# Row exponents of a gated delta-rule layer: from TensorE products to a trip through device memory

## The chip, the core and the metric

The kernel runs on one core of a Trainium2 chip. The metric is device time in microseconds (us) of one execution. The core has a matrix engine (TensorE, PE in the profile, with PEld for its weight loads), VectorE (DVE), ScalarE (ACT), GpSimd (POOL), a queue processor (SyncE, SP) and 16 DMA engines. Each engine works through its own list of instructions in order, and semaphores hold it where another engine's or a transfer's result is needed. DMA is issued from SP and from POOL here.

## The reference, cut to what matters

The model is a bidirectional encoder with two layers over 512 tokens of width 1024: first gated delta rule, then gated linear attention, each followed by an MLP. The change touches the delta-rule layer alone. It has 8 heads and two directions; each direction is computed in chunks:

```python
decay_mat = exp(where(causal, gc[..., :, None] - gc[..., None, :], -inf))
a_mat = where(strict, einsum('bhncd,bhnsd->bhncs', k * beta, k) * decay_mat, 0)
sol = triangular_solve(a_mat + eye, concat([v * beta, k * beta * exp(gc)]))
qk = einsum('bhncd,bhnsd->bhncs', q, k) * decay_mat
q_dec = q * exp(gc)
...
v_new = u_c - w_c @ state
o = q_dec @ state + qk @ v_new
```

`gc` is the running sum of log decays in a chunk. Every entry of `decay_mat` needs an exponent that belongs to its row plus one that belongs to its column, and `q_dec` needs one factor for each token.

## The kernel before, in words

Tokens are cut into 4 chunks of 128 (`NT = 4`, `P = 128`). `gdn` makes 8 `GdnHead` objects and emits, for step i, `recur` (the recurrence) of head i-2, `solve` of head i-1, `project` with `rows` of head i, and `finish` of head i-2. This is only the order in which code is written. A scheduler then merges the instructions into one list for each engine, by priorities and its own estimate of when things are ready; those lists are fixed in the program. Three heads are thus in work at once.

- `project` makes k, q, v and a gate z of the head: 24 products each (`pjk`, `pjq`, `pjv`, `pjz`), of a split weight `wh`, `wl` with a split x. Weights come through `wst` (3 buffers) on the SP queue.
- `rows` transposes k and q (`ktp`), sums their squares and makes, with tokens on partitions, the exponents: `rw` holds for each token, chunk and direction the exponent of its row, `cj` that of its column.
- `solve` makes k k^T (`kk`) and the decay matrix `E`, transposed: partition is the column's token, the free axis the row's. So `rw` is needed along the free axis and the same on all 128 partitions. Before, it is split into three bf16 parts (`rs`), transposed on TensorE (`rtp`, copied to `rt`, 6 x 512), and spread over the partitions by a product with the selector `sel` (`ep`, one PSUM bank per direction). From `ep` ScalarE makes exp for q (`qd`), then a second product adds the mask `mi` (-1e30 where the row is not later) to the same bank, and ScalarE makes `E`, with `cj` as its bias, in 8 pieces of 128 x 128. `E` times `kk` is `at`, its half-precision form `ath`, the 4 x 4 diagonal blocks `a4`; the solve starts with the products `hp` and goes on by doubling block sizes (`lv`, casts into `pz` and `Dd`), then `nw`, and `qk` (times `E`: `qke`).
- `recur` runs the states through products `m1`, `m2`, `m3` with ScalarE and VectorE between them, and makes the output `op`. `finish` normalises it on ScalarE (`fo`), transposes it on TensorE (`otp`) and applies the gate.

The PSUM pool has 8 banks: `ch` 2, `pj` 3, `tp` 1, `ac` 2; `ep`, `hp`, `lv`, `nw` and `qk` use the two of `ac`.

Of the kernel before, what the change touches and what calls it, by code (L numbers as in the profile page):

```python
# [17 lines left out]
P = 128  # L18
S = 512
# [1104 lines left out]
class GdnConst:  # L1124


    def __init__(self, c, pool, w_in, a_log, dt_bias, conv_w, norm_g, x):
        self.c, self.pool = c, pool
# [46 lines left out]
    def masks(self):  # L1175
        c, pool = self.c, self.pool
        G = c.nc.gpsimd
        self.idb = pool.tile([P, P], BF16, name="idb", bufs=1)
        G.tensor_copy(self.idb, c.ident)
# [3 lines left out]
        sf = pool.tile([6, 2, P], F32, name="self", tag="E", bufs=2)  # L1183
        G.memset(sf, 0.0)
        for s in range(3):
            G.affine_select(out=sf, in_=sf, compare_op=ALU.not_equal, fill=1.0, base=-2 * s,
                            pattern=[[-1, 2], [0, P]], channel_multiplier=1)
# [141 lines left out]
def gdn(c, w_in, conv_w, a_log, dt_bias, norm_g, w_out, ln_g, ln_b, x, w_next):  # L1329
    tc, nc = c.tc, c.nc  # L1330
    with c.banks(ch=2, pj=3, tp=1, ac=2), tc.tile_pool(name="gdn", bufs=1) as pool:
        g = GdnConst(c, pool, w_in, a_log, dt_bias, conv_w, norm_g, x)
# [9 lines left out]
        def load_z(hf):  # L1342
            if hf:
                tl = pool.tile([P, NT, S], F32, name="z", tag="sil", bufs=3)
            else:
                tl = heads[-1].next.kq
                more = [heads[-1].t2(tag, n).rearrange("p n i -> p (n i)") for tag, n in (("kt", 3), ("qd", 4))]
# [30 lines left out]
class GdnHead:  # L1378
# [75 lines left out]
    def rows(self, done):  # L1454
# [21 lines left out]
        rw = c.small.tile([P, NT, 2], F32, name="rw", tag="rw")  # L1476
# [4 lines left out]
        rs = c.small.tile([P, NT, 6], BF16, name="rsp", tag="rsp")  # L1481
        r1 = c.small.tile([P, NT, 2], F32, name="r1", tag="r1")
        V.tensor_copy(rs[:, :, 0:2], rw)
        V.tensor_tensor(r1, rw, rs[:, :, 0:2], ALU.subtract)
        V.tensor_copy(rs[:, :, 2:4], r1)
        V.tensor_tensor(r1, r1, rs[:, :, 2:4], ALU.subtract)
        V.tensor_copy(rs[:, :, 4:6], r1)
        rtp = self.bank("rtp", BF16, tag="tp")
        for n in range(NT):
            T.transpose(rtp[:6, n, :], rs[:, n, :], g.idb)  # L1490
        self.rt = pool.tile([6, S], BF16, name="rt", tag="rt", bufs=2)
        A.copy(self.rt, rtp[:6, :, :].rearrange("p n i -> p (n i)"))
# [17 lines left out]
    def solve(self, done):  # L1510
# [11 lines left out]
        eps, self.qd = [], []  # L1522
        for d in range(2):
            ps = self.bank("ep")
            T.matmul(ps, g.sel[:, d, :], self.rt, start=True, stop=True)
# [3 lines left out]
            self.qd.append(x)  # L1529
            eps.append(ps)  # L1530
# [7 lines left out]
        with c.in_order(mybir.EngineType.PE):  # L1538
            for d in (1, 0):
                T.matmul(eps[d], g.idb, g.mi[d].unsqueeze(1).to_broadcast([P, NT, P]), start=False, stop=True, skip_group_check=True)  # L1540
        for d, ps in enumerate(eps):
            e = self.t2("E", 2)
# [266 lines left out]
```

## Time and profile before

| | |
|---|---|
| runs | 1338.26, 1338.63, 1339.11 us |
| median | 1338.63 us |
| profiled execution | 1339.1 us as recorded with the trace |
| its span, first to last instruction | 1335.5 us |
| TensorE's mean granted clock | 0.997 of full speed |
| busy over the span: PE, DVE, ACT, POOL | 98%, 82%, 60%, 9% |
| moved by DMA | 154.35 MB, mean 116 GB/s |

The page gives busy times of the engines, groups of equal instructions with the idle time ahead of them and what ended it, the DMA issues with the time from issue to landing, and the chain of work that ended last. L with a number is a line of the kernel. A duration of a matmul is from its start to its modelled end; matmuls overlap, so that the distance between two starts tells what one of them costs the engine. The delta layer takes about 410 us of the span, and the rest (two MLPs and the linear attention) is the same code before and after.

### The profile page before, as it was taken

The numbers are of one execution on the slowest core, as the hardware profiler recorded it, in microseconds if no ns is written. First come the engines' busy times: TensorE is split into PE (matmuls) and PEld (weight loads), VectorE is DVE, ScalarE is ACT, GpSimd is POOL, SyncE is SP. The second block draws the span as 40 slices with busy tenths as digits, with TensorE's granted clock in tenths as the row PEclk, the third lists the DMA queues.
The fourth block names the chain that finished last, engine by engine and source line by source line (L and its number), as shares of the span: only waits on it lengthen the run. The fifth ranks groups of instructions, "written<-read, shape, count | busy, mean of one in ns | idle before, by whom it ended". The sixth has DMA issues, their size and how long they took to land.

```text
span 1335.5 us, 22220 instructions
## 1 busy us (share of the span) xinstructions
PE 1313.2 (98%) x8629; PEld 1122.0 (84%) x8629; DVE 1097.8 (82%) x1802; ACT 800.3 (60%) x1590; POOL 124.2 (9%) x177
## 2 busy tenths in 40 slices
PE   9999999999999999999999999999999999999996
PEld 8777787787777989999998888888889899999985
DVE  7797877888768878989988887967879679989888
ACT  4767666767643655666566754654456466566656
POOL 4000000000000910100102100000001001101011
PEclk9999999999999999999999999999999999999998
DMA  6221111211232684775748542222327476767566
GB/s 184 67 68 40 47 48 48 64 37 68 72 96 74 201 174 140 164 183 148 165 126 176 137 119 64 64 64 64 95 64 201 120 185 138 161 172 147 155 138 146
DMA packets 155660, 154.35 MB, mean 116 GB/s; under 512 B 7723, under 2 KB 122531, under 8 KB 155555
## 3 DMA queue, kind: packets, MB, share of 16 engines
q1 hardware_dynamic: 143779, 110.85, 28.1%
q0 software_dynamic: 11776, 42.08, 16.1%
q8 instruction: 68, 1.11, 0.3%
q14 instruction: 37, 0.30, 0.1%
HBM read 113.99 MB, written 2.10 MB: 87 GB/s over the span
## 4 chain that ended last, share of the span: by engine, by line
PE 87%; DVE 5%; ACT 5%; issue 1%; DMA 1%; DVEq 0%; POOL 0%; ACTq 0%; POOLq 0%
PE pX L123 3%; PE pX L122 3%; PE pX L124 3%; PE fx L124 3%; PE fx L123 3%; PE fx L122 3%; PE pjv L122 3%; PE pjv L123 3%; PE pjv L124 3%; PE m L1699 3%; PE pj L123 3%; PE pj L124 3%; PE pj L122 3%; PE fyz L122 2%; PE fyz L124 2%; PE fyz L123 2%
## 5 line engine op out<-in xcount | busy, mean ns | idle before, releaser
L96 ACT CAST wh<-wst 128x1024 fp32r<-128x1024 f32 x150 | 157.5, 1050 | 106.7 <-PE fyz L123 31.4
L101 DVE TENSOR_TENSOR wl<-wst,wh 128x1024 fp32r<-128x1024 f32 x148 | 182.3, 1232 | 46.4 <-ACT wh L96 45.4
L101 DVE TENSOR_TENSOR w2l<-w2r,w2h 128x1024 fp32r<-128x1024 f32 x92 | 112.3, 1220 | 28.4 <-ACT w2h L96 28.3
L96 ACT CAST w2h<-w2r 128x1024 fp32r<-128x1024 f32 x94 | 98.4, 1048 | 56.7 <-PE pX L124 24.8
L401 POOL DMA_DIRECT2D w2r<-w2r x56 | 48.4, 891 | 500.5 <-DVE w2l L101 176.3
L96 ACT CAST ah<-h 128x1024 fp32r<-128x1024 f32 x56 | 58.8, 1050 | 51.8 <-PE pZ L123 23.2
L450 DVE TENSOR_TENSOR wst<-wst 128x512 f32<-128x512 f32 x110 | 73.0, 682 | 0.2
L101 DVE TENSOR_TENSOR al<-h,ah 128x1024 fp32r<-128x1024 f32 x56 | 68.4, 1221 | 5.2 <-ACT ah L96 5.2
L123 PE MATMUL pX<-w2l,ah 128*128 128x512 f32 x168 | 66.2, 394 | 0.0
L122 PE MATMUL pX<-w2h,ah 128*128 128x512 f32 x168 | 66.0, 393 | 0.0
L124 PE MATMUL pX<-w2h,al 128*128 128x512 f32 x168 | 65.7, 391 | 0.0
L123 PE MATMUL pj<-xtl,wh 128*128 128x256 f32 (+1 forms) x192 | 64.7, 338 | 0.2 <-DVE xtl L188 0.2
L124 PE MATMUL pj<-xth,wl 128*128 128x256 f32 (+1 forms) x192 | 64.5, 337 | 0.0
L122 PE MATMUL pj<-xth,wh 128*128 128x256 f32 (+1 forms) x192 | 64.3, 337 | 0.1
L122 PE MATMUL pjv<-wh,xth 128*128 128x512 f32 x128 | 54.4, 425 | 0.0
L124 PE MATMUL pjv<-wh,xtl 128*128 128x512 f32 x128 | 50.2, 392 | 0.0
L123 PE MATMUL pjv<-wl,xth 128*128 128x512 f32 x128 | 50.0, 391 | 0.0
L124 PE MATMUL fx<-xh,wl 128*128 128x256 f32 x176 | 49.8, 283 | 0.0
L124 PE MATMUL fyz<-xh,wl 128*128 128x256 f32 x176 | 49.7, 282 | 0.0
L122 PE MATMUL fyz<-xh,wh 128*128 128x256 f32 x176 | 49.7, 282 | 0.0
L124 PE MATMUL fx<-xth,wl 128*128 128x256 f32 x176 | 49.7, 282 | 0.0
L123 PE MATMUL fx<-xtl,wh 128*128 128x256 f32 x176 | 49.7, 282 | 0.0
(528 smaller groups left out, 4303.5 us busy)
## 6 DMA issues: line engine op xcount, KB each, us to landing
wst<-in_mlp_w SPq DMA_DIRECT2D x68, 512.0 KB, 5.1
w2r<-in_mlp_w SPq DMA_DIRECT2D x60, 512.0 KB, 4.4
w2r<-w2r POOLq DMA_DIRECT2D x56, 512.0 KB, 5.6
wst<-in_a_w_in SPq DMA_DIRECT2D x32, 512.0 KB, 4.1
wst<-in_b_w_in SPq DMA_DIRECT2D x32, 256.0 KB, 3.1
wst<-in_a_w_out SPq DMA_DIRECT2D x8, 512.0 KB, 3.6
wst<-in_b_w_in SPq DMA_DIRECT2D x8, 512.0 KB, 4.0
wst<-in_b_w_out SPq DMA_DIRECT2D x8, 512.0 KB, 3.7
```

The source lines that it names most:

```text
L96: h = nc.scalar.copy(hi, src)
L101: self.halves = h, nc.vector.tensor_tensor(lo, src, hi.bitcast(F32), ALU.subtract)
L122: mm(ps, ah, bh, start=start, stop=False, **kw)
L123: mm(ps, ah, bl, start=False, stop=False, **kw)
L124: self.last_mm = mm(ps, al, bh, start=False, stop=stop, **kw)
L401: nc.gpsimd.dma_start(blocks[a + (q,)], blocks[b + (q,)], accum_op=ALU.add)
L450: plus = lambda a, b: V.tensor_tensor(a, a, b, ALU.add)
L1699: T.matmul(ps[:, d, :], *ops(d), start=True, stop=True)
```

## The change

The exponents no longer pass TensorE. SP copies the mask, which lies in device memory four times over (`later`, made and written once at the start), into `E`, and writes `rw` element by element as 8 rows of 128 into a small buffer in device memory (`row`). POOL then issues two transfers, each of which reads those 8 rows once for every partition: the first adds them onto the mask in `E`, the second puts them into `qd` as they are. ScalarE's exponentials work in place on `E` and `qd`. `qd` is one tile for both directions; its product with q becomes one VectorE instruction. The split into bf16 parts, the transposes, the copy `rt` and the four products per head are gone, with `sel`, `idb` and `mi`. A load of x late in the layer gets another half of a `qd` tile.

```diff
 class GdnConst.masks
-        self.sel = pool.tile([6, 2, P], BF16, name="sel", bufs=1)
-        G.tensor_copy(self.sel, sf)
-        self.mi = [pool.tile([P, P], BF16, name=f"mi{d}", bufs=1) for d in range(2)]
+        later = pool.tile([P, 2, P], F32, name="later", bufs=1)
         for d in range(2):
-            t = pool.tile([P, P], F32, name="tri", tag="cf", bufs=2)
-            self.tri(t, d, False, 0.0, NEG)
-            G.tensor_copy(self.mi[d], t)
+            self.tri(later[:, d, :], d, False, 0.0, NEG)
+        self.later = self.dram.tile([P, 2, NT, P], F32, name="laterd", bufs=1)
+        for n in range(NT):
+            G.dma_start(self.later[:, :, n, :], later)
...
 GdnHead.rows
-        rw = c.small.tile([P, NT, 2], F32, name="rw", tag="rw")
+        rdn = c.small.tile([P, 2, NT], F32, name="rw", tag="rw")
+        rw = rdn.rearrange("p d n -> p n d")
...
-        V.tensor_copy(rs[:, :, 0:2], rw)
-        V.tensor_tensor(r1, rw, rs[:, :, 0:2], ALU.subtract)
-        V.tensor_copy(rs[:, :, 2:4], r1)
-        V.tensor_tensor(r1, r1, rs[:, :, 2:4], ALU.subtract)
-        V.tensor_copy(rs[:, :, 4:6], r1)
-        rtp = self.bank("rtp", BF16, tag="tp")
-        for n in range(NT):
-            T.transpose(rtp[:6, n, :], rs[:, n, :], g.idb)
-        self.rt = pool.tile([6, S], BF16, name="rt", tag="rt", bufs=2)
-        A.copy(self.rt, rtp[:6, :, :].rearrange("p n i -> p (n i)"))
+        row = g.dram.tile([2 * NT, P], F32, name="row", tag="row", bufs=3)
+        self.e = pool.tile([P, 2, NT, P], F32, name="E", tag="E", bufs=2)
+        self.qd = pool.tile([P, 2, NT, P], F32, name="qd", tag="qd", bufs=2)
+        c.nc.sync.dma_start(self.e, g.later)
+        with c.nc.allow_non_contiguous_dma("one column to a row"):
+            c.nc.sync.dma_start(row.rearrange("u p -> p u"), rdn.rearrange("p d n -> p (d n)"))
+        every = row.rearrange("u p -> (u p)").partition_broadcast(P)
+        c.nc.gpsimd.dma_start(self.e.rearrange("p d n i -> p (d n i)"), every, accum_op=ALU.add)
+        c.nc.gpsimd.dma_start(self.qd.rearrange("p d n i -> p (d n i)"), every)
...
 GdnHead.solve
-        for d in range(2):
-            ps = self.bank("ep")
-            T.matmul(ps, g.sel[:, d, :], self.rt, start=True, stop=True)
-            x = self.t2("qd", 4)
-            A.activation(x, ps, AF.Exp)
-            V.tensor_tensor(x, self.kq[:, 1, :].rearrange("p (n i) -> p n i", n=NT), x, ALU.mult)
+        x = self.qd
+        A.activation(x, x, AF.Exp)
+        V.tensor_tensor(x, self.kq[:, 1, :].rearrange("p (n i) -> p n i", n=NT).unsqueeze(1).to_broadcast([P, 2, NT, P]),
+                        x, ALU.mult)
...
-        with c.in_order(mybir.EngineType.PE):
-            for d in (1, 0):
-                T.matmul(eps[d], g.idb, g.mi[d].unsqueeze(1).to_broadcast([P, NT, P]), start=False, stop=True, skip_group_check=True)
-        for d, ps in enumerate(eps):
-            e = self.t2("E", 2)
+        for d in range(2):
+            e = self.e[:, d, :, :]
             for n in range(NT):
-                A.activation(e[:, n, :], ps[:, n, :], AF.Exp, bias=self.cj[:, n, d:d + 1])
+                A.activation(e[:, n, :], e[:, n, :], AF.Exp, bias=self.cj[:, n, d:d + 1])
```

The scheduler makes new lists. Three places of them follow; the numbers behind names tell tiles apart.

On TensorE, where head 5's `kk` and head 3's `otp` stand, the list of before has the two selector products (`ep`, with the loads of `sel`) between `otp` and `kk`:

```order
L1757 MATMUL otp_3536<-ident_70,fo_3531 128x128
L1525 LDWEIGHTS sel_355
L1525 MATMUL ep_3654<-rt_3431,sel_355 128x512
L1525 LDWEIGHTS sel_355
L1525 MATMUL ep_3659<-rt_3431,sel_355 128x512
L122 MATMUL pjq_3977<-xth_107,wh_3973 128x512
L123 MATMUL pjq_3977<-xtl_108,wh_3973 128x512
L1699 MATMUL m2_3552<-vt_3550,xf_3305 128x128 x2
L1519 MATMUL kk_3649<-sil_2858 128x128 x4
```

and the list of now, at the same `otp` of head 3, goes on to the recurrence (`m2`) at once:

```order
L123 MATMUL pjk_3814<-xtl_110,wh_3810 128x512
L124 MATMUL pjk_3814<-xth_109,wl_3811 128x512
L1741 MATMUL otp_3421<-ident_70,fo_3416 128x128
L122 MATMUL pjk_3814<-xth_109,wh_3810 128x512
L1741 MATMUL otp_3421<-ident_70,fo_3416 128x128 x2
L123 MATMUL pjk_3814<-xtl_110,wh_3810 128x512
L1741 MATMUL otp_3421<-ident_70,fo_3416 128x128
L1683 MATMUL m2_3437<-vt_3435,xf_3197 128x128 x2
```

The products for the exponents are gone, and `kk` of head 5 now stands ahead of `otp`, 24 rows above it.

On ScalarE at the same place, from head 5's `neg` to its exponentials, the list of before:

```order
L197 ACTIVATE rsy_3521<-rsy_3521 128x4
L96 CAST wh_4100<-wst_4098 128x1024
L1492 COPY rt_3431<-rtp_3426 6x512
L1753 ACTIVATE fo_3531<-op_3017,ors_3519 128x128 x4
L1402 ACTIVATE sil_3475<-pjk_3941,cw_304 128x512
L1687 COPY vt_3550<-ktp_3545 128x512
L1527 ACTIVATE qd_3656<-ep_3654 128x512
```

and the list of now:

```order
L1496 ACTIVATE fq_3324<-c0_3325,bias2_79 128x4
L196 ACTIVATE rsy_3406<-oss_3398,bias1_77 128x4
L96 CAST wh_3929<-wst_3927 128x1024
L1435 COPY sil_3360<-pjz_3372 128x512
L197 ACTIVATE rsy_3406<-rsy_3406 128x4
L1671 COPY vt_3435<-ktp_3430 128x512
L1528 ACTIVATE E_3312<-E_3312,cj_3309 128x128 x6
L1515 ACTIVATE qd_3313<-qd_3313 128x1024
L1737 ACTIVATE fo_3416<-op_2921,ors_3404 128x128 x4
L1528 ACTIVATE E_3312<-E_3312,cj_3309 128x128 x2
```

The exponentials of `E` and `qd`, which stood behind head 3's `fo`, now stand ahead of it; heads 4 and 6 have the same rows.

On SP, whose list held weight loads alone at this place of the layer, the copies of the mask and the writes of the exponents now stand between them (heads 3 to 5 here):

```order
L1481 DMA row_2115<-rw_2112 128x8x1
L1479 DMA E_2714<-laterd_353 128x1024
L50 DMA wst_3329<-in_a_w_in 128x8x128
L50 DMA wst_3366<-in_a_w_in 128x8x128
L1481 DMA row_2713<-rw_2710 128x8x1
L50 DMA wst_3808<-in_a_w_in 128x8x128
L50 DMA wst_3844<-in_a_w_in 128x8x128
L1479 DMA E_3312<-laterd_353 128x1024
```

The mask of a head is copied two weight loads ahead of the head's exponents, and the two adding and plain transfers of each head stand on POOL with nothing between them.

More of the change, by code (lines that the diff above doesn't have):

```diff
@@ L1346, in load_z @@
                 tl = heads[-1].next.kq
-                more = [heads[-1].t2(tag, n).rearrange("p n i -> p (n i)") for tag, n in (("kt", 3), ("qd", 4))]
+                more = [heads[-1].t2("kt", 3).rearrange("p n i -> p (n i)"),
+                        pool.tile([P, 2, S], F32, name="qd", tag="qd", bufs=2)[:, 0, :]]
             for t in range(NT):
@@ L1732, in recur @@
             mm = [(self.qke[d][:, n, :], vns[d][n]) for d in range(2)]
-            mm += [(self.qd[d][:, n, :], states[d][n]) for d in range(2) if states[d][n] is not None]
+            mm += [(self.qd[:, d, n, :], states[d][n]) for d in range(2) if states[d][n] is not None]
             for i, (l, r) in enumerate(mm):
```

21 lines of the change are left out of this document (5 added, 16 removed).

## The prediction

> **What bounds the kernel now.** I read the page first, then the stretches of the layer that changes, then its groups of instructions and the engines' timelines. The profiled execution spans 1335.5 us and took about 1339.1; the median of the runs is 1338.63, so sums go against that median without a correction.
>
> ```profile
> span 1335.5 us, 22220 instructions
> PE 1313.2 (98%) x8629; PEld 1122.0 (84%) x8629; DVE 1097.8 (82%) x1802; ACT 800.3 (60%) x1590; POOL 124.2 (9%) x177
> ```
>
> The delta layer runs from 0 to about 410 us, a head every 43 us. Two of its stretches (busy us of PE, weight loads, VectorE, ScalarE, GpSimd; clock; DMA share; GB/s):
>
> ```profile
> 120.00:165.00 45.00, 44.05 (x415) 35.63 (x415) 39.92 (x84) 30.32 (x87) 0.00 (x0) 1.00 0.19 50
> 255.00:300.00 45.00, 44.86 (x398) 36.18 (x397) 37.15 (x86) 30.36 (x87) 0.00 (x0) 1.00 0.14 38
> ```
>
> TensorE is busy for 98% of each at full clock, GpSimd idle, DMA under a fifth used. So a microsecond taken off TensorE's list is worth a microsecond, and one in which it must wait costs one.
>
> **What the change removes.** Per head four small transposes (`rtp`), two products with the selector and two that add the mask (`ep`); five short VectorE operations and the copy `rt`. Durations in the groups overlap, so I price the matmuls by distances between starts, from TensorE's timeline of head 5:
>
> ```profile
> 257.46 0.39 PE L1490 MATMUL rtp<-idb,rsp 128*6 128x128 bf16 x4
> 257.78 0.50 PE L124 MATMUL pjk<-xth,wl 128*128 128x512 f32 x1
> 258.11 0.40 PE L122 MATMUL pjq<-xth,wh 128*128 128x512 f32 x1
> 258.35 0.39 PE L123 MATMUL pjq<-xtl,wh 128*128 128x512 f32 x1
> ...
> 260.46 0.60 PE L1525 MATMUL ep<-rt,sel 6*128 6x512 bf16 x2
> 261.00 0.50 PE L122 MATMUL pjq<-xth,wh 128*128 128x512 f32 x1
> 261.33 0.39 PE L123 MATMUL pjq<-xtl,wh 128*128 128x512 f32 x1
> ...
> 264.49 0.59 PE L1540 MATMUL ep<-mi,idb 128*128 128x512 bf16 x2
> 264.73 0.58 PE L124 MATMUL pjq<-xth,wl 128*128 128x512 f32 x1
> 265.15 0.69 PE L1699 MATMUL m<-r,xf 128*128 128x128 f32 x4
> ```
>
> `rtp` holds the engine 0.32 us, the selector pair 0.54, the mask pair 0.24 and 0.19 more before the next start (0.42 against a steady 0.23). After each interruption the first projection takes 0.33 instead of 0.23: twice 0.10. Sum 1.49 per head, 11.9 for eight. Some interruptions merge with others that stay, so I take 1.41 per head: **-11.3 us**. VectorE's and ScalarE's removed work gains nothing by itself: neither is full, and what TensorE then waits for is below.
>
> **What it adds on the queues.** Per head: the mask's copy (512 KB) and the exponents' write (1024 elements of 4 bytes) on SP; an adding transfer into `E` and a plain one into `qd` (512 KB each) on POOL. The copy waits for `E` of two heads before, and weight loads stand behind it; they have room:
>
> ```profile
> SPq L50 <- DVE wl L101: 686.1, 111, 23.6
> ```
>
> SP spends 686 us waiting for buffers, so loads are issued far ahead, and I cost the copies and the stops at nothing; were a stop as long as the longest wait (23.6 us), the cover would be gone. On POOL nothing stands behind these transfers until the norm's parameters after the last head. The mask's four writes at the start share the DMA engines with the first loads of x: 0 to 2.8 us (512 KB at the 186 GB/s of 0 to 35 us), 0.3 taken, since they are small beside 6 MB. `qd`'s exponential and product become one of double size each: nothing.
>
> **The new path.** Today `rw` becomes `E`'s input on TensorE. Then it is: write, wait for landing, adding transfer, wait for landing. No row shows either; the nearest DMA issues (KB, us from issue to landing):
>
> ```profile
> gst<-in_b_w_in SPq DMA_DIRECT2D x1, 128.0 KB, 2.4
> out<-xt SPq DMA_DIRECT2D x4, 256.0 KB, 3.2
> gb<-in_b_gate_b POOLq DMA_DIRECT2D x1, 4.0 KB, 5.9
> ln<-in_ln_b POOLq DMA_DIRECT2D x2, 512.0 KB, 4.4
> h<-wst POOLq DMA_DIRECT2D x2, 512.0 KB, 4.7
> wl<-wst POOLq DMA_DIRECT2D x2, 512.0 KB, 6.0
> ```
>
> The write lies between 2.4 (`gst`, 128-byte pieces read) and 5.9 (`gb`, 1024 separate elements, but beside heavy loads); I take 2.8, nearest to the two quiet SP rows. The adding transfer lies between 4.4 (a row repeated for all partitions, not added) and 6.0 (added); I take 4.6, since the DMA engines are nearly idle here. With 0.2 for two hand-overs, `E` is there **7.6 us after `rw`** (bounds 7.0 and 12.1).
>
> Is that early enough? The exponentials of head 5 ran 11.5 us after `rw`:
>
> ```profile
> 253.57 0.17 DVE L1479 SCALAR_TENSOR_TENSOR rw<-lnr,gc 128x8 f32<-128x8 f32 x1 [0.24 <-ACT lnr L1472]
> ...
> 259.00 1.10 ACT L1753 ACTIVATE fo<-op,ors 128x128 f32<-128x128 f32 x4
> 265.12 0.88 ACT L1544 ACTIVATE E<-ep,cj 128x128 f32<-128x128 f32 x3 [1.14 <-PE ep L1540]
> ```
>
> So `E` for itself is in time. But ScalarE works in order, and the new order puts six exponentials of `E` and the whole of `qd` ahead of `fo` (the output of two heads before) in heads 4, 5 and 6; in head 5 `fo` now runs 5.4 us after `rw`, before any of them. TensorE's transposes of `fo` (`otp`) cannot be passed by. When are they due? In the new order head 5 has, from the transposes of q to `otp`, 30 projections, 24 products `lv`, 24 half-precision products `nw`, 8 transposes, and the four products each of `qk` and `kk`.
>
> ```profile
> 249.29 0.40 PE L1605 MATMUL lv<-Xd,pz 128*128 128x64 f16 x8
> 249.62 0.66 PE L1464 MATMUL ktp<-ident,sil 128*128 128x128 f32 x4
> 251.20 0.22 PE L1651 MATMUL nw<-Dd,ath 128*128 128x128 f16 x1 [0.22 <-ACT Dd L1640]
> 251.31 0.22 PE L1651 MATMUL nw<-Dd,ath 128*128 128x128 f16 x1
> 262.00 1.06 PE L1519 MATMUL kk<-sil 128*128 128x128 f32 x8
> 262.90 0.61 PE L1699 MATMUL m<-vd,kt 128*128 128x128 f32 x4
> ```
>
> That is 30 x 0.23 + 7 restarts of 0.10 + 24 x 0.03 + 24 x 0.056 (a pair, of which one is shown, every 0.11) + 8 x 0.11 + 8 x 0.225 = 12.4 us. `rw` comes 3.95 us after those transposes (249.62 to 253.57), so `otp` is due at `rw` + 8.5, its last at + 9.1. On ScalarE after 7.6: six `E` at 0.27 (1.6), `qd` 1.1, `fo` 1.1: done at 11.4. **Late by 2.3.** For the other heads the distance from the transposes to `rw` differs:
>
> ```profile
> 42.97 0.66 PE L1464 MATMUL ktp<-ident,sil 128*128 128x128 f32 x4
> 45.66 0.18 DVE L1479 SCALAR_TENSOR_TENSOR rw<-lnr,gc 128x8 f32<-128x8 f32 x1 [0.77 <-ACT lnr L1472]
> 70.05 0.63 PE L1464 MATMUL ktp<-ident,sil 128*128 128x128 f32 x4
> 73.33 0.17 DVE L1479 SCALAR_TENSOR_TENSOR rw<-lnr,gc 128x8 f32<-128x8 f32 x1
> 199.64 0.53 PE L1464 MATMUL ktp<-ident,sil 128*128 128x128 f32 x3
> 203.54 0.17 DVE L1479 SCALAR_TENSOR_TENSOR rw<-lnr,gc 128x8 f32<-128x8 f32 x1 [0.30 <-ACT lnr L1472]
> 286.67 0.38 PE L1464 MATMUL ktp<-ident,sil 128*128 128x128 f32 x2
> 289.77 0.16 DVE L1479 SCALAR_TENSOR_TENSOR rw<-lnr,gc 128x8 f32<-128x8 f32 x1
> ```
>
> Head 4 has the same 12.4 us (25 projections, 72 `lv`, 20 `nw`) and the same 3.9: late by 2.3. Head 6 has the list of head 5 and 3.1: late by 1.5. In head 1 three `E` stand ahead of the cast `Dd` that ends head 0's solve; its products come after 29 projections, 72 `lv`, 8 transposes and `kk`, 11.3 us, less 3.3: due at `rw` + 8.0. `Dd` is done at 7.6 + 0.8 + 0.8 + 0.1 = 9.3: late by 1.3. In head 0 the first `hp` comes after 67 projections, 4 transposes and `kk`, 16.9 us, less 2.7: due at `rw` + 14.2. Ahead of it run six `E` (1.6), `qd` (1.1), a cast (0.6), two `E` (0.5), a scaling and two casts (0.7, 1.0, 0.7) and VectorE's `a` (0.4), 6.6 in all: 14.2, just in time. Heads 2, 3 and 7 have over 1 us to spare by the same count. Waits: 2.3 + 2.3 + 1.5 + 1.3 = **+7.4 us**. Beyond 7.6 each further microsecond of the path costs five, one for each of these heads.
>
> Sum: -11.3 + 7.4 + 0.3 = -3.6, so **1335.0 us**. With the path's lower bound 7.0 the waits shrink by 4 x 0.6 to 5.0: 1332.6. With 12.1 they are 7.4 + 5 x 4.5 = 30: 1358.
>
> **Rules of the Trainium skill.** The 512 KB rows from POOL take 4.4 to 6.0 us. The Trainium skill, "DMA: Bandwidth & Descriptors", section "Anatomy of one DMA", fits 2.0 us plus the bytes over 436 GB/s, an estimate of 3.2 us for such a transfer and 2.0 for the small one; by it the path were 5.4 us and the sum near 1327.6. The trace's rows are longer than that fit. The same page, "Specifications", says that pieces under 512 bytes are read, modified and written; the `gst` row (128-byte pieces into SBUF) shows no such penalty, and no run here shows 4-byte writes to device memory. It speaks against the change.
>
> **Rivals.**
> (B) *The transfers are short and nothing waits.* With the path at or below 5.3 us `fo` of head 4 is ready when due (5.3 + 3.8 = 9.1), and only the saving is left: 1338.6 - 11.3 + 0.3 = 1327.6. For it: GpSimd and DMA idle here. Against it: its two transfers would have to beat 2.4 and 4.4 together by 1.5 us. Chance 0.13.
> (C) *The write of single elements is slow.* 1024 scattered 4-byte writes, and the same 4 KB read 128 times with an addition, could take the upper rows, 3.5 to 5.9 and 4.7 to 6.0. From a path of 8.3 us on (7.6 plus 3.6 / 5) the change loses; at 9.9 the waits are 19 and the time 1346.6. For it: `gb`, the only row with 1024 separate elements, 5.9. Against it: `gb` ran among other loads. Chance 0.33.
> (D) *The time saved turns idle.* Every head's solve is a chain over three engines, and VectorE is at 37 to 40 of 45 us; if that chain sets the pace, the saving and the waits hide in each other: 1338 to 1339. Against it: TensorE's idle time here is under 1 us per head. Chance 0.12.
>
> **How the numbers follow.** Forecast (path of 7.0 to 8.2 us, 1332.6 to 1338.0) 0.42, B 0.13, C 0.33, D 0.12. About what a measurement can tell from no change is 0.2%, 2.7 us: faster is below 1335.9, a path under 7.8. Of the forecast 0.33 lies there and 0.09 within. Faster: 0.33 + 0.13 = 0.46; same: 0.09 + 0.12 + 0.01 of C = 0.22; slower: 0.32. The range takes in B but its lowest part, and C up to a path of about 9.8: 1328 to 1346; beyond lie some 0.2.
>
> **What would show it.** TensorE busy less by 11 us in 35 to 400 us, with its rows L1490, L1525 and L1540 gone. `row` landing near 2.8 us and `E<-row` near 4.6. ScalarE idle ahead of `E`, put down to a DMA, in every head, and TensorE's idle time before `otp` in heads 4 to 6, before `nw` in head 1, 7.4 us in all. A `row` landing over 3.6 us, or stalls in heads 2, 3 or 7, would make the prediction wrong to the slow side; no idle time before `otp` would to the fast one.

## The result: 1439.9 us, and the profile after

The changed kernel takes 1439.9 us (four runs, 1437.5 to 1442.4) against 1338.5 of the kernel before on the same chip: a ratio of 1.076, interval 1.0747 to 1.0773. The forecast was 1335.0 with a range of 1328 to 1346. The profiled execution of after spans 1437.1 us at a mean granted clock of 0.961 (before 1335.5 and 0.997).

Busy times of the page after:

```profile
PE 1323.0 (92%) x8565; PEld 1134.1 (79%) x8565; DVE 1095.6 (76%) x1754; ACT 796.9 (55%) x1574; POOL 135.4 (9%) x189
```

64 matmuls are gone, as the change says. Yet TensorE is busy for longer, and for a smaller share. Two stretches of the layer, with the columns of the stretches shown before (busy us of PE, weight loads, VectorE, ScalarE, GpSimd; clock; DMA share; GB/s):

```profile
120.00:165.00 45.00, 35.66 (x340) 28.95 (x338) 31.18 (x62) 26.49 (x79) 1.40 (x2) 0.92 0.32 83
300.00:345.00 45.00, 29.20 (x219) 24.05 (x218) 24.07 (x53) 20.25 (x67) 1.40 (x2) 0.81 0.28 59
```

TensorE, busy 98% before, works 29 to 36 of 45 us, and its clock falls. What it waits for (us in total, times, longest), from the list of waits of TensorE in 0 to 520 us, first of before (to 420) and then of after:

```profile
PE nw L1651 <- ACT Dd L1640: 1.8, 4, 0.6
...
PE otp L1757 <- ACT fo L1753: 0.6, 1, 0.6
```

```profile
PE otp L1741 <- ACT fo L1737: 42.5, 3, 15.0
PE m L1683 <- ACT vd L1698: 28.3, 3, 9.8
PE nw L1635 <- ACT Dd L1624: 12.2, 4, 10.4
PE hp L1544 <- DVE a L1533: 9.1, 1, 9.1
```

Four products, each waiting for ScalarE (or VectorE behind it), 92.1 us in all against 2.4 before. And why ScalarE is late, from the list of waits of all engines, and the DMA issues (KB, median us to landing):

```profile
ACT E L1528 <- DMA E<-row: 91.5, 7, 17.5
```

```profile
E<-laterd SPq DMA_DIRECT2D x8, 512.0 KB, 11.6
E<-row POOLq DMA_DIRECT2D x8, 512.0 KB, 7.4
...
row<-rw SPq DMA_DIRECT2D x8, 4.0 KB, 11.7
```

The write took 11.7 us where I had put 2.8, the adding transfer 7.4 for 4.6. The 7.4 is a median of unlike heads: 4.9 and 5.0 us in heads 0 and 1, and 9.0, 8.7 and 8.7 in heads 4 to 6. In those three the mask copy of the next head and weight loads were under way beside it. In head 5 two loads and the copy had been issued at 308.1, 310.7 and 311.9, while the write was on its way; the first load landed at 320.6 and the copy at 324.6. Head 5 shows the whole chain on its timeline (start, duration; idle time before and its end in brackets):

```profile
305.48 0.17 DVE L1474 SCALAR_TENSOR_TENSOR rw<-lnr,gc 128x8 f32<-128x8 f32 x1 [0.45 <-ACT lnr L1466]
305.68 0.37 SPq L1481 DMA_DIRECT2D row<-rw  x1
318.05 0.85 POOL L1483 DMA_DIRECT2D E<-row  x1 [59.77 <-DMA row<-rw]
318.60 0.84 POOL L1484 DMA_DIRECT2D qd<-row  x1
326.78 1.86 ACT L1528 ACTIVATE E<-E,cj 128x128 f32<-128x128 f32 x6 [17.47 <-DMA E<-row]
328.54 1.04 ACT L1515 ACTIVATE qd<-qd 128x1024 f32<-128x1024 f32 x1
329.49 1.10 ACT L1737 ACTIVATE fo<-op,ors 128x128 f32<-128x128 f32 x4
...
329.89 0.48 PE L1741 MATMUL otp<-ident,fo 128*128 128x128 f32 x1 [14.96 <-ACT fo L1737]
```

From `rw` to the first exponential pass 21.3 us. Read in the same way, heads 0 to 6 need 17.0, 17.8, 18.5, 17.6, 21.6, 21.3 and 21.1 (forecast 7.6). ScalarE stands idle for 17.5 us, `fo` (head 3's, long ready) stands behind, and TensorE waits 15.0 us for it.

The clock is a loss of its own. The stretches around that wait:

```profile
310.00:315.00 5.00, 4.93 (x32) 3.76 (x28) 3.56 (x8) 0.00 (x0) 0.00 (x0) 1.00 0.37 22
315.00:320.00 5.00, 0.00 (x0) 0.00 (x0) 0.00 (x0) 0.00 (x0) 1.40 (x2) 0.79 0.75 130
320.00:325.00 5.00, 0.00 (x0) 0.00 (x0) 0.00 (x0) 0.00 (x0) 0.00 (x0) 0.50 1.08 297
325.00:330.00 5.00, 0.11 (x1) 0.11 (x2) 0.39 (x1) 3.22 (x10) 0.00 (x0) 0.50 0.21 78
330.00:335.00 5.00, 5.00 (x18) 4.32 (x19) 3.24 (x5) 2.77 (x11) 0.00 (x0) 0.51 0.00 0
335.00:340.00 5.00, 5.00 (x30) 4.26 (x29) 4.20 (x11) 3.83 (x10) 0.00 (x0) 1.00 0.00 0
```

In idleness the clock goes to 0.50 and stays there for the first 5 us of new work: 18 matmuls in 330 to 335, 30 in the next 5 us. The Trainium skill, "TensorE: Matmul & The Clock Gate", section "Part 1: The HAM clock gate", under "What's actually happening", says that the array runs at half its clock after an idle window of about 3.4 us and needs about as much of sustained work to get it back; this trace agrees on the half clock and on the fall: a mean of 0.79 in 315 to 320, from 1.00 to 0.50, puts it at 317.9, 3.0 us after the last matmul. The way back took 5 us of work here, longer than that figure.

The account: waits +89.7 us, TensorE's busy time +9.8 (1313.2 to 1323.0), 99.5 of the 101.6 us by which the span grew. That busy time holds both a saving and a slowing. The run `prev` below has the same number of matmuls at a clock of 0.994:

```profile
PE 1305.9 (97%) x8565; PEld 1120.1 (83%) x8565; DVE 1093.1 (81%) x1754; ACT 796.9 (59%) x1575; POOL 135.4 (10%) x189
```

So 7.3 us are saved, and 17.1 lost to the slow clock. Both are a little low: prev has 5 us of work at clock 0.50 too, behind its wait in head 0, which is by estimate 2.5 us of busy time. The saving is then nearer 10 us and the loss nearer 20.

### The profile page after: what moved, and what is told of

It is laid out like the page before. It is cut to its first block, busy times and chain, and to the rows that moved or that the text cites. A ratio compares the mean times of both kernels' runs of the same rounds, so it can differ in the third digit from the quotient of the medians.

```text
span 1437.1 us, 22115 instructions
## 1 busy us (share of the span) xinstructions
PE 1323.0 (92%) x8565; PEld 1134.1 (79%) x8565; DVE 1095.6 (76%) x1754; ACT 796.9 (55%) x1574; POOL 135.4 (9%) x189
## 4 chain that ended last, share of the span: by engine, by line
PE 76%; DMA 10%; ACT 6%; DVE 6%; issue 1%; POOL 0%; DVEq 0%; POOLq 0%; ACTq 0%; SPq 0%
DMA row<-rw 5%; PE pX L122 3%; PE pX L124 3%; PE pX L123 3%; PE fx L124 3%; PE fx L123 3%; PE fx L122 3%; PE m L1683 3%; PE pjv L122 3%; PE pjv L123 3%; PE pjv L124 3%; DMA E<-row 3%; PE pj L123 3%; PE pj L124 3%; PE pj L122 2%; PE fyz L122 2%
## 5 line engine op out<-in xcount | busy, mean ns | idle before, releaser
L1528 ACT ACTIVATE E<-E,cj 128x128 f32<-128x128 f32 x64 | 20.4, 393 | 91.5 <-DMA E<-row 91.5
L123 PE MATMUL pX<-w2l,ah 128*128 128x512 f32 x168 | 66.1, 393 | 0.0
L1516 DVE TENSOR_TENSOR qd<-sil,qd 128x1024 f32<-128x1024 f32 x8 | 9.8, 1223 | 60.6 <-ACT qd L1515 60.6
L123 PE MATMUL fx<-xl,wh 128*128 128x256 f32 x176 | 49.8, 283 | 0.0
## 6 DMA issues: line engine op xcount, KB each, us to landing
E<-laterd SPq DMA_DIRECT2D x8, 512.0 KB, 11.6
```

The costliest lines, as they stand in the source:

```text
L123: mm(ps, ah, bl, start=False, stop=False, **kw)
L1528: A.activation(e[:, n, :], e[:, n, :], AF.Exp, bias=self.cj[:, n, d:d + 1])
```

## The experiments

Theories ahead of them: (1) the 1024 single elements make the write slow; (2) SP's ring does, where it stands among other loads; (3) the adding is slow; (4) work that stands behind the exponentials on ScalarE turns the trip into TensorE's waits one for one; its rival is that the head's own chain takes the time.

**w32: the block written as 128 pieces of 32 bytes.**

```diff
-        row = g.dram.tile([2 * NT, P], ...)
+        row = g.dram.tile([P, 2 * NT], ...)
-            c.nc.sync.dma_start(row.rearrange("u p -> p u"), rdn...)
+        c.nc.sync.dma_start(row, rdn...)
```

> The exponents' block in device memory is written as 128 pieces of 32 bytes (partition by partition) in place of 1024 single elements of 4 bytes; read back as before by both transfers. The exponents thus reach E and qd in a permuted order, and the mask's kept entries hold -1000 in place of 0, so that nothing overflows: the values are others, the work is the same. Theory 1 (the 1024 single elements make the write slow): `row` lands in about 3 us in place of 11.7, the path from `rw` to `E` falls from 17 to 22 us to about 10, and by five waits for each of the 8.5 us the time falls by 40 us or more, to 1400 or less. Theory 2 (the write is slow because it lies on SP's ring among loads of masks and weights): `row` still lands in 9 us or more, and the time stays at 1430 to 1445. Theory 3 (the adding transfer is the slow part): `row` short, but the time only a little lower, since `E<-row` keeps 7.4.

1358.8 us, ratio 1.0157 (1.0142 to 1.0172): 81 us of the 101 are gone. Its DMA issues and TensorE's waits:

```profile
E<-row POOLq DMA_DIRECT2D x8, 512.0 KB, 6.0
...
row<-rw SPq DMA_DIRECT2D x8, 4.0 KB, 1.4
```

```profile
PE otp L1740 <- ACT fo L1736: 11.4, 3, 4.3
PE m L1682 <- ACT vd L1697: 4.6, 2, 2.6
PE nw L1634 <- ACT Dd L1623: 3.7, 4, 2.0
PE hp L1543 <- DVE a L1532: 2.7, 1, 2.7
```

The same four waits, 22.4 us for 92.1, with the path at 8.5 to 10.6 us in heads 0 to 6. Theory 1 in its outcome; the theory that adding is what is slow would have kept `E<-row` at 7.4. The masks' copies land in 5.2 us here in place of 11.6, though nothing but the form of the write has changed on their queue: the slow write held up other transfers as well.

**poolq: the write issued by POOL.**

```diff
-            c.nc.sync.dma_start(row.rearrange("u p -> p u"), ...)
+            c.nc.gpsimd.dma_start(row.rearrange("u p -> p u"), ...)
```

> The write of the exponents, element by element as before, is issued by POOL in place of SP, on the queue of the two transfers that read it. Results are the same. Theory 1 (single elements): `row` keeps 10 us or more, the time stays near 1440; the loads on SP behind it (wst of w_out, masks) land sooner than now (10.0 and 11.6). Theory 2 (SP's ring): `row` lands in 3 to 6 us and the time falls to 1400 or less. Theory 3 (adding transfer): no change of time, 1435 to 1445.

1442.9 us, ratio 1.0784 (1.0768 to 1.08); `row` lands in 10.1 us, so theory 2 falls. The masks' copies on SP land in 5.7 us in the median, but that is the early heads: those of heads 4, 5 and 7 still take 13.8, 16.7 and 12.8, and `E<-row` takes 8.4. So transfers on the other queue than the write's land late too. TensorE's own wait for weights stays at the 1.8 us of before.

**plain: no mask copy, no addition.**

```diff
-        c.nc.sync.dma_start(self.e, g.later)
-        c.nc.gpsimd.dma_start(self.e..., every, accum_op=ALU.add)
+        c.nc.gpsimd.dma_start(self.e..., every)
```

> The mask's copy is left out and the first transfer writes the exponents into E without adding; the column's exponents are held at -60 or lower, so that nothing overflows (no mask: the values are others). Theory 3 (adding is slow): `E<-row` falls from 7.4 to 4.5 or less, and at five waits for each of the 3 us the time falls to about 1425. Theories 1 and 2: `E<-row` stays at 6 to 8 and the time at 1435 to 1445, or some 5 us lower where the copies' traffic is what made the write late.

1419.6 us, ratio 1.0607 (1.0589 to 1.0624); `row` 10.9, `E<-row` 6.0. The time is 20 us less, below both forecasts; the four products wait 73.7 us for 92.1, which is 18 of the 20. Head by head, theory 3 is worth some 1.2 us. In heads 0 and 1, where no mask copy runs beside it in either kernel, the plain transfer takes 3.8 and 3.7 us and the adding one of after 4.9 and 5.0. In heads 4 to 6 the difference is 3.2, 1.6 and 1.2, and there the mask copies are gone as well. This run doesn't tell the two apart.

**prev and start: nobody waits for a fresh block.** In prev the transfers read the block of the head before, in start one made at the beginning; the writes stay.

```diff
-        every = row.rearrange(...)
+        g.rows = [*getattr(g, "rows", [row]), row]
+        every = g.rows[-2].rearrange(...)       # prev
+        every = g.fixed.rearrange(...)          # start
```

> Both transfers of a head read the block written for the head before (head 0 reads its own); every write and transfer stays, only nobody waits for the fresh block. The exponents are another head's, and the mask's kept entries hold -1000, so the values are others. If the wait for write and read-back is the cause (theories 1 to 3 alike), the time falls to that of before less TensorE's saving, 1325 to 1335, with the granted clock back at 1.00 and TensorE busy over 97% of 75 to 400 us. If the traffic itself costs (loads late behind the writes, DMA shared), 1345 or more stays, with TensorE waiting for weights.

> As the run in which both transfers read the block of the head before, but all heads, the first too, read a block made at the start (all entries -1; the mask's kept entries hold -1000): every write and transfer stays and nobody waits for a fresh block. In that earlier run head 0 still waited for its own block, and TensorE was busy for 28.8 of 40 us in 35 to 75 us. If the wait is the whole loss, those 11 us go and the time is 1328 to 1335, faster than before (TensorE's saving of 11.3 us, less what the mask's writes at the start cost). If the traffic costs by itself (loads behind the slow writes), 1340 to 1346 stays.

prev: 1345.1 us, ratio 1.0052 (1.0037 to 1.0067); start: 1337.1, ratio 0.999 (0.9981 to 0.9999). prev misses 1325 to 1335 and stands where its rival, the traffic, begins, but not for the rival's reason: TensorE waits 2.0 us for weights (before 1.8), and its one long wait is head 0's `hp`, 10.3 us. prev, where head 0 alone still waits, and then a later head:

```profile
35.00:75.00 40.00, 28.83 (x152) 22.48 (x150) 19.84 (x42) 20.00 (x46) 2.93 (x4) 0.89 0.51 111
...
255.00:300.00 45.00, 44.31 (x409) 36.33 (x409) 40.90 (x87) 33.16 (x99) 1.39 (x2) 1.00 0.42 95
```

TensorE is full again from head 1 on at clock 1.00, while `row` still takes 11.1 us to land: a slow write that nobody waits for cost TensorE next to nothing here (`forms` below shows a case where it does cost). start missed its forecast for a reason of its own making: its early transfers let `qd`'s exponential move into the start of the kernel, where ScalarE's casts of x stood behind it:

```profile
ACT qd L1519 <- DMA qd<-fixed: 8.3, 1, 8.3
```

Head 0's `rw` comes 8.6 us later than in before (54.22 for 45.66). Without those 8.3 us it would be at 1329, near the 1327.6 of the rival without waits; that is an estimate, and gcearly4 below is the run that shows the gain.

**t512: one transpose, 8 rows of 512 bytes.**

```diff
+        T.transpose(rtp, rdn.rearrange("p d n -> p (d n)"), c.ident)
+        A.copy(rt, rtp)
+        c.nc.sync.dma_start(row, rt)
```

> Results are the same. The exponents are transposed by one TensorE product (128 x 8 to 8 x 128), copied by ScalarE and written as 8 rows of 512 bytes in place of 1024 single elements. Theory 1 (single elements): `row` lands in 2 us or less, the path is 9 to 11 us (transpose and copy 0.8, write 1.5 to 2, adding transfer 6), and the time is that of the run with 32-byte pieces plus little, 1355 to 1365: still slower than before, since adding transfer and ScalarE's order remain. If pieces under 512 bytes were what hurts in that run too, `row` falls further below its 1.4 us and the time to 1350 or less.

1360.7 us, ratio 1.0165 (1.0151 to 1.0179), as with 32-byte pieces: fewer and larger pieces gain nothing further. The landing of `row` isn't in this trace; the path, with transpose and copy in it, is 9.0 to 11.0 us in heads 0 to 6.

**half: 512 elements.**

```diff
-        row = g.dram.tile([2 * NT, P], ...)
+        row = g.dram.tile([NT, P], ...)
-            c.nc.sync.dma_start(..., rdn.rearrange("p d n -> p (d n)"))
+            c.nc.sync.dma_start(..., rdn[:, 0, :])
```

> 512 single elements are written in place of 1024 (one direction's exponents, which both halves of E and qd then read; the mask's kept entries hold -1000; the values are others, the sizes of the two transfers are the same). Theory 1 (each single element costs a fixed time): from 128 pieces in 1.4 us and 1024 in 11.7, one piece costs 11.5 ns, and 512 land in 5.8 us; the path falls by 6 us in all eight heads, and the time by 45 to 50, to about 1392. If the landing has a fixed cost for non-contiguous writes that does not go with their count, `row` stays at 10 us or more and the time above 1425.

1435.2 us, ratio 1.0725 (1.0707 to 1.0743); `row` lands in 9.3 us. Half the elements save 2.4 us of 11.7: theory 1 as a price per element is wrong.

**forms and forms2: one more write in each head, each of another form, read by nobody.** In each, one line a head like these:

```diff
+        c.nc.sync.dma_start(t.rearrange("u p -> p u"), flat[:, 0:1])  # formc: t [1, P]
+        c.nc.sync.dma_start(t[:, 0:1], flat[:, 0:1])                  # formf: t [P, P]
```

> The kernel whose row exponents come early (one part known for all heads, k normalised by a product with ones) with one more write in each head that nobody reads, each of another form, from the same `rw` tile: head 0 forma, 1024 single elements as 8 rows of 128; head 1 formb, 512 (4 rows); head 2 formc, 128 (one row); head 3 formd, 1024 single elements each 64 bytes from the next; head 4 forme, 128 pieces of 32 bytes; head 5 formf, 128 single elements 512 bytes apart; head 6 formg, 256 (2 rows); head 7 formh, 512 pieces of 8 bytes (4 rows of 128 pairs). Results are the same. Theory 1a (a price for each piece and a fixed one, from the two runs 6.9 us + 4.7 ns x pieces): forma 11.7, formb and formh 9.3, formg 8.1, formc, forme and formf 7.5; formd as forma. But forme was 1.4 in an earlier run, so 1a needs the size of the piece too. Theory 1b (single elements that lie beside each other in memory get into each other's way): formd lands in 5 us or less, formf in 2 or less, formc above formf, forma and formb as before.

> The fastest version with early exponents, with one more write in each head that nobody reads, all of 128 pieces (one for each partition) but the last: formp, formq, formr, forms 4 bytes each, 8, 16, 32 and 64 bytes apart; formt 4 bytes each, side by side; formu 8 bytes and formv 16 bytes each, side by side; formw 512 single elements 64 bytes apart. Results are the same. Known so far, for 128 pieces: 4 bytes side by side 8.7 us, 4 bytes 512 bytes apart 1.4, 32 bytes side by side 1.4. If pieces that share a line of 32 bytes get into each other's way: formr, forms and formw 1.4 to 2, formp near 4 to 6, formq 2 to 4, formu 4 to 5, formv 2 to 3, formt 8 to 9. If the line has 64 bytes, formr is slow too (2 to 3). If the size of a piece alone counted, all of 4 bytes would take 8 to 9.

The DMA issues of the two (KB, us to landing; forma and formd have no landing in the trace, nor formp and forms):

```profile
formb<-rw SPq DMA_DIRECT2D x1, 2.0 KB, 8.3
formc<-rw SPq DMA_DIRECT2D x1, 0.5 KB, 8.7
...
forme<-rw SPq DMA_DIRECT2D x1, 4.0 KB, 1.4
formf<-rw SPq DMA_DIRECT2D x1, 0.5 KB, 1.4
formg<-rw SPq DMA_DIRECT2D x1, 1.0 KB, 9.3
formh<-rw SPq DMA_DIRECT2D x1, 4.0 KB, 4.0
```

```profile
formq<-rw SPq DMA_DIRECT2D x1, 0.5 KB, 2.8
formr<-rw SPq DMA_DIRECT2D x1, 0.5 KB, 4.0
...
formt<-rw SPq DMA_DIRECT2D x1, 0.5 KB, 8.8
formu<-rw SPq DMA_DIRECT2D x1, 1.0 KB, 4.1
formv<-rw SPq DMA_DIRECT2D x1, 2.0 KB, 2.9
```

128 elements of 4 bytes take 8.7 us side by side and 1.4 us 512 bytes apart; 128, 256 and 512 side by side take 8.7, 9.3 and 8.3. So the number of pieces counts little (1024 took 11.7) and a small size alone doesn't make a write slow; what does is that small pieces lie beside each other: theory 1b in its outcome. Its line of 32 bytes is not borne out, though. Some of these writes had a load of 512 KB ahead of them on SP, and their pieces left late; the packet records of the two traces tell when the last piece had left, and the landing comes 6.1 to 8.2 us after that for 4 bytes side by side (formc, formg, formt; some 4 to 5 for formb, whose pieces left more slowly), 1.8 for 128 pieces of 8 bytes (formu) and 2.7 for 512 (formh), 0.4 to 0.5 for 16 bytes side by side (formv) and for 4 bytes 16 apart (formq), 0.4 to 0.8 for what lies 32 bytes or more apart (forme, formf, formr). formw, 512 elements 64 bytes apart, fits no better than halfway: 4.4 us, some 2.5 of it after its last piece. A stretch of after shows that it is not the sending that takes the time. Head 0's write is issued at 47.3 and lands at 59:

```profile
49.00:50.00 1.00, 1.00 (x6) 0.83 (x5) 0.00 (x0) 0.37 (x1) 0.00 (x0) 1.00 1.18 240
50.00:51.00 1.00, 1.00 (x6) 0.83 (x5) 0.28 (x1) 1.00 (x2) 0.00 (x0) 1.00 0.19 1
51.00:52.00 1.00, 1.00 (x6) 0.81 (x5) 1.00 (x2) 0.27 (x1) 0.00 (x0) 1.00 0.00 0
```

The DMA engines are done by 51 and then idle (share 0.00, to 53) while the write has not landed. That the memory takes close pieces one after another is an inference from these rows.

The run `forms` shows besides that such a write can cost time though nobody reads it. It took 1347.3 us (one run), 8 more than gcearly below, on which it is built. Its forma, 1024 elements side by side, went off at 47.3, and head 0's adding transfer beside it took 12.8 us (53.2 to 66.1) where gcearly's took 7.2; `hp` of head 0 then waited 12.9 us for 5.6.

The Trainium skill, "DMA: Bandwidth & Descriptors", section "Specifications", says that pieces under 512 bytes are read, modified and written. By the landing the pieces under 512 bytes are not alike here: 4-byte pieces 512 bytes apart and 32-byte pieces side by side both land in 1.4 us.

**hold, hold2, t512hold: the exponentials moved on ScalarE.** hold puts E's and qd's exponentials of a head behind `fo` of two heads before; hold2 behind the last `vd` of the head before; t512hold is t512 with hold.

```diff
+        with c.tc.issue_after(self.prev.prev.fo.ins):     # hold; hold2: self.prev.lastvd
             A.activation(x, x, AF.Exp)
```

> Results are the same. The exponentials of E and qd of a head are held on ScalarE behind `fo` of two heads before (from head 2 on); the transfers stay as they are. Theory 4 (ScalarE's order makes TensorE wait at `otp`): the waits of `otp` on `fo` (88 us in the list of waits) go, the next late product is `hp`, which is due about 12 us after `otp` and 8 us after E: late by 6 to 8 us where `otp` was late by 14, so some 6 x 7 = 40 us less, 1390 to 1410. Rival (the head's own chain from E on sets the pace, whatever stands behind on ScalarE): the wait moves to `hp` or `m` in full and the time stays at 1430 to 1445.

> Results are the same. The exponentials of E and qd of a head are held on ScalarE behind the last `vd` of the head before, so that neither `fo` nor `vd` stands behind them; by then, some 20 us after `rw`, the trip through device memory is over. Theory 4 (what hurts is that other heads' work stands behind the exponentials on ScalarE): nothing waits behind them, but E is some 9 us later in the head's own chain than before; with 34 us from E to the end of the solve and 14 us of recurrence ahead of the next head's E, a head takes 48 in place of 43 us: 1370 to 1385. Rival (the head's own chain already takes all of the 58 us that a head now needs): 1425 to 1445, no better than with `fo` alone ahead.

> Results are the same. Both mends at once: the exponents transposed and written as 8 rows of 512 bytes (alone 1360.7), and the exponentials of E and qd behind `fo` of two heads before (alone 1431.9). With the short path of 9 to 10 us, E is ready about when the kernel before ran it, so theory 4 (the rest of the loss is work queued behind the exponentials) expects that only head 0 still waits (57.4 for 51.8 us) and a little else: 1335 to 1345. Rival (the rest is the head's own chain): 1355 to 1362, as with the rows alone.

hold: 1431.9 us, ratio 1.0694 (1.0679 to 1.0708), against 1390 to 1410. The 88 us of its forecast were 42.5 of the products `otp` and 45.1 of their weight loads, the same waits counted twice. Taken alone it looked like the rival, but its list of waits says otherwise:

```profile
PE m L1687 <- ACT vd L1702: 64.1, 6, 12.6
PE nw L1639 <- ACT Dd L1628: 11.7, 5, 9.8
```

`otp` no longer waits; `vd` now stands behind the exponentials, and the product `m` waits for that. hold2, with neither behind them, takes 1367.5 us, ratio 1.0221 (1.0206 to 1.0236), 72 us less than after with the same write and the same transfers, and below its forecast of 1370 to 1385. The trip from `rw` to `E` is shorter there too (14.6 to 18.6 us for 16.9 to 21.5), but in heads 1 to 7 `E` lies ready for 10 us and more before ScalarE takes it, so that is not what saves the time. So the loss was mostly work queued behind the exponentials, theory 4. What hold2 still loses is at both ends, at head 0 (30.52 of 40 us busy in 35 to 75) and where the last head's late solve has nothing beside it:

```profile
400.00:420.00 20.00, 15.13 (x124) 10.89 (x122) 10.68 (x20) 5.50 (x19) 2.15 (x4) 1.00 0.51 145
420.00:450.00 30.00, 22.49 (x103) 16.85 (x102) 17.79 (x47) 7.64 (x29) 0.00 (x0) 0.89 0.00 1
```

t512hold: 1354.3 us, ratio 1.0118 (1.0102 to 1.0133), a miss against 1335 to 1345: only 6 us below t512, since `m` waits for `vd` there again (10.6 us).

**gcearly and its four successors: nothing waits for the trip.** The part of the row exponent that comes from the running sums of log decays is known for all heads at 41 us. It is written to device memory once and read by each head's two transfers long before use (head 0's excepted). The part from k's norm goes through one product with ones:

```diff
+        c.nc.gpsimd.dma_start(self.e..., every(g.gr), accum_op=ALU.add)
+        c.nc.gpsimd.dma_start(self.qd..., every(g.er))
+        A.activation(sq, kq[:, 0, :], AF.Square)
+        T.matmul(ns, g.onr, sq, start=True, stop=True)
+        A.activation(kn, ns, AF.Ln, bias=c.bias[RMS_EPS])
+        A.activation(kn, kn, AF.Exp, scale=-0.5)
+        V.tensor_tensor(kn, kn, kq[:, 0, :], ALU.mult)
-            T.matmul(kk[:, n, :], self.kc(n), self.kc(n), ...)
+            T.matmul(kk[:, n, :], self.kc(n), self.kn[:, n * P:(n + 1) * P], ...)
```

> Results are the same up to rounding. The row exponent is split: its part from the running sums of log decays, known for all heads at 41 us, is transposed once, written to device memory once for all heads (64 rows of 512 bytes, and their exponentials), and each head's adding and plain transfer read it long before they are needed. The part from the norm of k is known late and goes another way: squares of k times a matrix of ones on TensorE (one 128x512 product), Ln and Exp, and k so normalised is one side of `kk`. qd needs no exponential. If the wait for the trip was the whole loss, nothing waits for device memory, TensorE saves 1.49 - 0.33 us a head, 9 us in all, and the time is 1328 to 1332. If the added steps on ScalarE and VectorE ahead of `kk` (some 2 us) delay the solve, 1335 to 1342.

gcearly2 takes the sums for device memory straight from a product; gcearly3 moves `qd`'s product with q into the recurrence, and gcearly4 holds it there; gcearly5 is gcearly with the sums copied straight from PSUM and head 0's rows written first:

```diff
+                nc.tensor.matmul(gtp[:, d, :], self.yg[:, d, :, :]..., self.cum[d], ...)  # gcearly2 to 4
+            if step == 2:                                                                 # gcearly4
+                with c.tc.issue_after(rlast.ins):
+                    V.tensor_tensor(x, self.kq[:, 1, :]..., x, ALU.mult)
+            for n, rows in ((1, slice(0, 8)), (7, slice(8, 64))):                         # gcearly5
```

> Results are the same up to rounding. As the run with the early part of the exponent, but the sums for device memory come straight from a product of the gates with the triangle (already transposed), and their copies and writes stand right behind it: in that run head 0's `E` was ready at 58.5 us where before it was 51.8, because the copy of the sums stood behind VectorE's filters and the write went off at 46.8. Now the write should go off near 43, and head 0 gain 4 to 5 us: 1333 to 1336. If head 0's wait was not on the path, 1338 to 1340 stays.

> Results are the same up to rounding. As the run with early exponents and sums straight from the product, which took 1353.2 because VectorE's product of qd waited for its transfer (24.7 us, six times) with the solve's work behind it; that product now stands in the recurrence, later by most of a head. Head 0's E was ready at 50.6 us there. If that wait was the loss: TensorE saves 9 us and nothing waits, 1329 to 1335. If another order takes its place: 1338 or more.

> Results are the same up to rounding. As the run with early exponents, sums straight from the product and qd's product in the recurrence (1345.5), but that product is held on VectorE behind the recurrence's own work of its third step, when qd's transfer is long over. There VectorE waited 14.3 us for qd's transfer and TensorE 7.8 us for casts behind it. If those waits were the loss: 1331 to 1337. If the order of the lists makes other waits of the same size: 1341 or more.

> Results are the same up to rounding. As the first run with early exponents (1339.3), where the one long wait of TensorE was head 0's `hp` (5.6 us; E ran at 58.5 us): the copy of the sums now comes straight from PSUM, and head 0's 8 rows are written ahead of the other 56. E of head 0 should run near 53 and `hp` wait under 1 us: 1332 to 1336, faster than before. If the order changes with it and other waits take its place: 1338 to 1345.

gcearly: 1339.3 us, ratio 1.0006 (0.9997 to 1.0015); gcearly2: 1353.2, 1.0114 (1.0099 to 1.013); gcearly3: 1345.5, 1.0057 (1.0044 to 1.0069); gcearly5: 1347.1, 1.007 (1.0058 to 1.0083). gcearly2 and gcearly5 lie above both of their forecasts. Each of the four has a wait that before had not; three rows, of gcearly, gcearly2 and gcearly3 in this order:

```profile
PE hp L1559 <- DVE a L1548: 5.6, 1, 5.6
```

```profile
DVE qd L1533 <- DMA qd<-er: 24.7, 6, 5.7
```

```profile
PE lv L1603 <- DVE Dd L1622: 7.8, 5, 3.4
```

gcearly5 meant to mend the first and got the waits of the other two (20.8 and 8.1 us) with its new order. gcearly4, which holds VectorE's product of `qd` until its transfer is long over, takes **1331.6 us** against 1336.7 beside it, ratio 0.9961 (0.9947 to 0.9975): 0.4% faster than before, and faster than after. Its list of TensorE's waits has nothing left above what before had:

```profile
PE bap L147 <- DVE wh L165: 2.0, 1, 2.0
...
PE nw L1649 <- ACT Dd L1638: 1.2, 4, 0.5
```

## Why the prediction was wrong

- **The saving on TensorE** (-11.3 us) was real in kind: the rows are gone, and with the waits gone gcearly4 is 5.1 us faster than before. In size it was a little too high: gcearly4, whose clock doesn't fall in the layer, is busy 7.2 us less (1306.0 for 1313.2) with eight added products of 0.33 us, which makes 9.8 removed. In after it was hidden under the waits.
- **The path** is the step that failed: 7.6 us forecast, 17.0 to 21.6 measured in heads 0 to 6. The write was priced at 2.8 from rows that read from device memory or write long pieces. Its upper bound, `gb` (5.9), was a read of 1024 elements; no row of before had small pieces written side by side, so it was no bound at all. It took 11.7. The adding transfer took 7.4 for 4.6, past its upper bound of 6.0 too. That price was near for a transfer with little beside it (4.9 and 5.0 in heads 0 and 1, 5.1 in prev, where `qd`'s started later); what the prediction left out is the company of heads 4 to 6, 8.7 to 9.0 us at a DMA share of 1.08 in 320 to 325 us. The prediction's other estimate of the path, 5.4 with 2.0 for the write and 3.2 for the adding transfer, was further off.
- **The waits' mechanism was right, and its rows too.** With the measured paths the prediction's own rule gives 9.4 us at `hp` of head 0 (17.0 + 6.6 - 14.2; measured 9.1), 11.5 at `nw` of head 1 (17.8 + 1.7 - 8.0; 10.4), and 16.3, 16.0 and 15.0 at `otp` of heads 4 to 6, 47.3 in all (42.5). That alone would be 1338.6 - 11.3 + 0.3 + 68.2 = 1395.8.
- **The slope of five heads** was the second wrong step. Heads 2, 3 and 7 had "over 1 us to spare", which a path 12 us longer uses up: three more waits, `m` for `vd`, 28.3 us. In heads 2 and 3 they are of the same kind; in head 7 `vd` stands behind `qd`'s exponential, which waits 9.7 us for `qd`'s own transfer, and that transfer had no time in the sum. Stalls in these heads were named as what would show the prediction wrong on the slow side, and a `row` over 3.6 us too.
- **The clock** was not in the sum: 17.1 us more in busy TensorE. 1395.8 + 28.3 + 17.1 = 1441, against 1439.9. That it meets to 1 us is partly luck: the rule's waits are 6.2 us above the measured 62.0, and the 11.3 saved are 4.0 above the 7.3 that belong with the 17.1.
- **Mask copies and stops on SP at nothing**: right for the stops, since moving the write off SP (poolq) left the time as it was and TensorE's wait for weights stayed at 1.8 us. For the copies it was not shown to be right: held up by the write (11.6 us to landing), they run beside the adding transfers of heads 4 to 6, and plain, without copies and without adding, is 20 us faster.
- **Rivals.** C had the right mechanism and place; its 1346.6 came from a path of 9.9, and w32, whose path is of that length, took 1358.8. B (no waits) comes out only where no head waits for its own trip. D (saving and waits hide in each other) is not seen.

What stays open: what happens between the last piece and the landing is inferred from forms of writes, not seen; and how the 20 us of plain divide between the mask copies and the adding was not tried by itself.

## What to carry to other kernels

A trip through device memory cost much as latency here, and little as traffic, except where its slow write held up a transfer that somebody waited for. Look for the part of the data that is known early and send that, so that nothing waits for it. Before a wait is put on an engine that works in order, list what stands behind it: every one of those rows is late by the same amount, and moving one of them ahead only shows the next (otp, then m). Transpose on the chip, or write in pieces of 32 bytes and more, before a column goes to device memory.

## What the runs showed of the hardware

- Writes of 4 bytes side by side land in 8 to 12 us, almost whatever their number (128: 8.7; 1024: 11.7), 128 of them in 1.4 us when 512 bytes apart; 128 pieces of 32 bytes side by side in 1.4.
- Head 0's write in after landed well after its pieces had left: the DMA engines' share was 0.00 for 2 us of the 11.7.
- A slow write holds up transfers beside it: the masks' copies took 11.6 us, and 5.2 where the same 4 KB went in pieces of 32 bytes (w32).
- A wait of 9 to 15 us costs TensorE some 2 us beyond itself (17.1 us over eight such waits): the clock at 0.50 lasted into the first 5 us of new work.
